# One level of Strassen's recursion for the convolution branch of an encoder block, moved with two gate blocks into a stage of its own behind the heads

## The chip, the cores and the metric

The kernel runs on one core of one Trainium2 chip. The metric is the device time of one execution in microseconds (us). The core has five engines that work side by side, each in its own order: TensorE (PE in the profile, with its weight loads as PEld), VectorE (DVE), ScalarE (ACT), GpSimd (POOL) and SyncE (SP), which here issues nearly all DMAs.

## The reference

One block of a bidirectional encoder, sequence 1024, width 1024, float32. Cut to what matters:

```python
h = rmsnorm(x, norm_w) * (1 + scale) + shift            # scale, shift, gate from silu(c) @ w_ada
(a_bg, a_cg, a_x, a_z, q, k, v, z_b, a_raw, b_raw, gate_a_raw, gate_b_raw) = split(h @ w_in)
ya = a_cg * dwconv3(a_bg * a_x) * silu(a_z);  ya = ya @ w_pa
q, k, v = silu(dwconv5([q, k, v]))                      # q, k l2-normalised, 8 heads of 128
o = gated_delta(q, k, v, g, beta) + flip(gated_delta(flip ...))   # chunked scan, both directions
yb = (rmsnorm(o) * silu(z_b)) @ w_pb
merged = sigmoid(gate_a_raw) * ya + sigmoid(gate_b_raw) * yb
return rmsnorm(x + gate * (merged @ w_o), final_norm_w)
```

## The kernel before, in words

`h` is kept transposed in SBUF: 8 tiles of 128 features x 1024 tokens, each as a rounded high part `hhi[k]` and the rest `hlo[k]`. The columns of `w_in` are taken in blocks of 128; a block's weights are loaded, and split in the same way into `wh` (ScalarE copy) and `wl` (GpSimd subtraction). One block's product is two halves of 512 tokens; a half is 8 values of k times three matmuls (`wh*hhi`, `wh*hlo`, `wl*hhi`) of 128x128 by 512. So a block is 48 matmuls. There are 80 such blocks of `w_in`: ten groups of eight, named bg, cg, ax, az (the convolution branch), q, k, v, z (the heads), ga, gb (the two gates).

The stages, in order of time:

- Start: x is loaded and normed, the first blocks k0, q0, v0 and k1 are multiplied.
- Heads: for each of 8 heads the streams `prep_k`, `prep_q`, `chain` and `head_out` do the scan. `prep_k` makes the decay matrices `D` and `N` (two buffers each: head h waits for the end of `chain` of head h-2, the mark `chain_e`), inverts 32x32 blocks on GpSimd (`E`, 30 steps of two instructions) over a round trip through DRAM, and `chain` runs the 8 chunk steps with short matmuls (`psy`, `psz`, `cb`, `o`). `fill` is a stream of block products that TensorE does whenever the chain has nothing ready: the q, k, v, z blocks of the coming heads (27 behind q1), and between them 24 gate blocks: ga, gb and az, whose results go through `activated` to DRAM (`sga_d`, `sgb_d`, `sza_d`). `choose` picks: the first 6 gates at once (`START`), the last 4 at the end (`RESERVE`), the others spread evenly over the 27.
- The order within this stage is found by the class `Scheduler`, from estimated costs and due times; it emits the instructions of all engines in that order, and each engine keeps it (`manual_schedule`). Where instructions emitted outside such a region fall among them is left to the compiler's own scheduler.
- Convolution branch: for j in 0..7 the blocks bg, ax, cg (`wtile` loads and splits weights, `product` multiplies), the width-3 convolution on VectorE (L1140, L1142), the product with `sza_d` (L1156) and the split into `yhi[j]`, `ylo[j]` (L1157, L1158), which stay in SBUF. Beside it the gate column of w_ada (`wadag`, L1144, L1146).
- pa: `ya @ w_pa`, 8 blocks over `yhi`, `ylo`; the result times `sga` goes to `m_d`. Beside it `yb_d` is read back and split into `bhi`, `blo` (L1178, L1179).
- pb: `yb @ w_pb`, 8 blocks; merged with `m_d` into `mhi`, `mlo`.
- fo: `merged @ w_o`, residual, final norm, store.

PSUM is four pools of two banks, `pp`, `pg`, `pc`, `po`. SBUF tiles of a later stage lie on bytes of earlier ones, and wait for the last use of just those tiles.

Of the kernel before, what the change touches and what calls it, by code (L numbers as in the profile page):

```python
# [15 lines left out]
P = 128  # L16
# [9 lines left out]
RESERVE = 4  # L26
# [7 lines left out]
LO_POOL = (2, 5)  # L34

# [7 lines left out]
class Slot:  # L43
    """What was done to a part of a tile: ends of reads, writes and memsets, and instructions not issued yet."""
# [6 lines left out]
class Scheduler:  # L51
    """Orders the instructions of all engines by an estimate of when they can run.

    Instructions of the engines other than TensorE are kept until their operands are there by the estimate, and then
    go to their engine by priority. Streams are generators that ask for TensorE instructions, PSUM banks, tiles and
    each other's marks; the first of them goes on whose next instruction can start at once, or else the one that can
    start first."""
# [126 lines left out]
    def step(self, stream):  # L184
        """Does what a stream asks for, and goes on to what it asks for next."""
# [65 lines left out]
class Engine:  # L251
    """Hands an engine's instructions to the scheduler."""
# [31 lines left out]
def block(ctx: ExitStack, tc: tile.TileContext, x, cT, wada, wadag, badaT, nwT, win, wab, cva, cvq,  # L284
# [10 lines left out]
    wp = pool("wp", 2)  # L295
# [22 lines left out]
    sza_d = dr.tile([8, P, T], F32, name="sza_d")  # L318
# [27 lines left out]
    def kmul(ps, w, k, half):  # L346
        wh, wl = (t[:, ch(k)] for t in w)
# [42 lines left out]
    ctx.enter_context(tc.manual_schedule(engines={nc.tensor.engine}))  # L390
    hctx = ctx.enter_context(ExitStack())
# [648 lines left out]
    def fill():  # L1040
# [11 lines left out]
        gates += [(G_B + j, f"gb{j}", activated("gb", j, sgb_d, AF.Sigmoid), []) for j in range(8)]  # L1052
        gates += [(A_Z + j, f"az{j}", activated("az", j, sza_d, AF.Silu), []) for j in range(8)]
# [33 lines left out]
    def wtile(src, name):  # L1087
        with tc.high_priority():
            hi = wp.tile([P, KT * P], F32R, tag="whi", name=f"wh_{name}")
            lo = wp.tile([P, KT * P], F32R, tag="wlo", name=f"wl_{name}")  # L1090
            for q in range(2):
                raw = wp.tile([P, 512], F32, tag="wraw", name=f"wr_{name}_{q}")
                Q.dma_start(raw, src[:, ch(q, 512)])
                S.activation(hi[:, ch(q, 512)], raw, AF.Copy)  # L1094
                G.tensor_tensor(lo[:, ch(q, 512)], raw, hi[:, ch(q, 512)].bitcast(F32), ALU.subtract)  # L1095
        return hi, lo

    def product(w, mhi, mlo, half, name):
        ps = bank((pp, pg)[half], f"pp_{name}_{half}")
        for k in range(KT):  # L1100
            wh, wl = (t[:, ch(k)] for t in w)
            sl = ch(half, 512)
            PE.matmul(ps, wh, mhi[k][:, sl], start=k == 0, stop=False)  # L1103
            PE.matmul(ps, wh, mlo[k][:, sl], start=False, stop=False)  # L1104
            PE.matmul(ps, wl, mhi[k][:, sl], start=False, stop=k == KT - 1)  # L1105
        return ps


    yctx = ExitStack()
    yp = yctx.enter_context(tc.tile_pool(name="yp", bufs=1, reuse_waits="tile", side="right"))  # L1110
    yhi = [yp.tile([P, T], F32R, name=f"yhi{k}") for k in range(KT)]
    ylo = [yp.tile([P, T], F32R, name=f"ylo{k}") for k in range(KT)]
    with tc.tile_pool(name="ap", bufs=2, reuse_waits="tile") as ap:
# [226 lines left out]
```

## Time and profile before

| | us |
|---|---|
| median of 3 runs (range) | 1516.65 (1513.97 to 1516.81) |
| span of the profiled execution | 1511.0 |
| start, up to the block v1 | 196.2 |
| heads, up to the first bg matmul | 769.4 |
| convolution branch (24 blocks) | 263.0 |
| pa (8 blocks) | 90.3 |
| pb (8 blocks) | 88.7 |
| fo and the end | 103.4 |

The page gives no time of the profiled execution beside its span, from its first to its last instruction; the median of the runs is 5.65 us more than that span. The profile lists instructions by line and tile: `pp_bg<-hhi,wh_bg` is a matmul into the PSUM tile of block group bg from `hhi` and `wh_bg`. All instructions that the scheduler of the heads emits have L200 (TensorE) or L278 (others); so groups are told apart by tile.

### The profile page before, as it was taken

Reading aid. Unit: us, or ns where it says so; the run is one execution under the profiler, and the core shown is the slowest. Engines: PE = TensorE matmul, PEld = TensorE weight load, DVE = VectorE, ACT = ScalarE, POOL = GpSimd, SP = SyncE. Lnnn points to the kernel's source line nnn. Section 1 sums busy time; section 2 is a strip of 40 time slices with the busy share of each in tenths; the row PEclk is TensorE's granted clock in tenths of the full one; section 3 lists DMA queues with packets and bytes.
Section 4 is the critical chain, followed back from the end, with each engine's and each line's share of the span. In section 5 each row is a group of like instructions: output and inputs, shape, how many; then the busy total and the mean of one; then the engine's idle time right before and its main releaser. Section 6 shows DMA issues by size and latency. Waiting matters only on the chain.

```text
span 1511.0 us, 22593 instructions
## 1 busy us (share of the span) xinstructions
PE 1433.0 (95%) x8730; PEld 1196.2 (79%) x8730; DVE 735.0 (49%) x1382; ACT 549.8 (36%) x1308; POOL 645.2 (43%) x793
## 2 busy tenths in 40 slices
PE   5999999898999999989999999999999999999898
PEld 3787878787787878878878878888888888888686
DVE  7869334664853845647628422134443344122325
ACT  5226325663553654635535424211111112122211
POOL 6213894167184392671852931222222222355401
PEclk7899999999999999999999999999999999999999
DMA  8232332223314113222132121322222137344602
GB/s 327 83 109 64 112 98 57 71 70 98 84 44 134 35 56 127 57 78 84 59 103 70 57 84 44 125 97 80 74 86 96 56 120 256 133 130 143 229 20 98
DMA packets 90298, 149.15 MB, mean 99 GB/s; under 512 B 41424, under 2 KB 41808, under 8 KB 90192
## 3 DMA queue, kind: packets, MB, share of 16 engines
q1 hardware_dynamic: 89904, 146.94, 29.6%
q8 instruction: 68, 1.11, 0.3%
q10 hardware_dynamic: 288, 0.79, 0.1%
q14 instruction: 38, 0.31, 0.1%
HBM read 118.21 MB, written 29.49 MB: 98 GB/s over the span
## 4 chain that ended last, share of the span: by engine, by line
PE 54%; DVE 9%; POOL 8%; ACT 5%; DMA 4%; issue 2%; SPq 0%; POOLq 0%; ACTq 0%
PE pp_az L200 4%; PE pp_gb L200 3%; PE cb L200 3%; PE pp_k L200 3%; DMA mr<-m_d 2%; PE o L200 2%; POOL E L278 2%; PE pp_v L200 2%; POOL et L278 2%; PE pp_cg L1103 2%; PE pp_cg L1105 2%; PE pp_cg L1104 2%; PE pp_bg L1105 2%; PE pp_ax L1105 2%; PE pp_bg L1104 2%
## 5 line engine op out<-in xcount | busy, mean ns | idle before, releaser
L278 POOL TENSOR_TENSOR E<-E,et 64x30 f32<-64x30 f32 (+14 forms) x240 | 143.9, 600 | 17.1
L278 POOL TENSOR_TENSOR et<-E 64x30 f32<-64x30 f32 (+14 forms) x240 | 135.2, 564 | 17.2
L1138 DVE TENSOR_TENSOR axp<-pp_ax,bg 128x512 f32<-128x512 f32 x16 | 11.1, 692 | 111.1 <-PE pp_ax L1105 90.5
L278 ACT ACTIVATE vw<-cb,cols 128x128 f32<-128x128 f32 x112 | 36.2, 365 | 76.1 <-PE cb L200 75.7
L278 ACT ACT_TABLE_LOAD x47 | 60.3, 1283 | 1.6 <-PEq L1335 0.8
L278 DVE SCALAR_TENSOR_TENSOR vT<-xpad,cvq_t,vT 128x1024 f32<-128x1024 f32 x32 | 58.6, 1831 | 1.0
L1095 POOL TENSOR_TENSOR wl_ax<-wr_ax,wh_ax 128x512 fp32r<-128x512 f32 x16 | 27.3, 1724 | 68.2 <-ACT wh_ax L1094 68.2
L278 POOL TENSOR_TENSOR wl_q<-wr_q,wh_q 128x512 fp32r<-128x512 f32 x16 | 22.0, 1390 | 72.2 <-ACT wh_q L278 67.4
L200 PE MATMUL pp_z<-hhi,wl_z 128*128 128x512 f32 x128 | 52.2, 408 | 0.0
L200 PE MATMUL pp_z<-hhi,wh_z 128*128 128x512 f32 x128 | 52.2, 407 | 0.0
L200 PE MATMUL pp_gb<-hlo,wh_gb 128*128 128x512 f32 x128 | 51.9, 406 | 0.0
L200 PE MATMUL pp_ga<-hhi,wh_ga 128*128 128x512 f32 x128 | 51.8, 405 | 0.0
L200 PE MATMUL pp_gb<-hhi,wh_gb 128*128 128x512 f32 x128 | 51.8, 405 | 0.0
L200 PE MATMUL pp_z<-hlo,wh_z 128*128 128x512 f32 x128 | 51.7, 404 | 0.0
L200 PE MATMUL pp_az<-hhi,wl_az 128*128 128x512 f32 x128 | 51.7, 404 | 0.0
L200 PE MATMUL pp_az<-hhi,wh_az 128*128 128x512 f32 x128 | 51.7, 404 | 0.0
L200 PE MATMUL pp_gb<-hhi,wl_gb 128*128 128x512 f32 x128 | 51.6, 403 | 0.0
L200 PE MATMUL pp_az<-hlo,wh_az 128*128 128x512 f32 x128 | 51.4, 402 | 0.0
L200 PE MATMUL pp_ga<-hlo,wh_ga 128*128 128x512 f32 x128 | 51.3, 401 | 0.0
L200 PE MATMUL pp_ga<-hhi,wl_ga 128*128 128x512 f32 x128 | 51.2, 400 | 0.0
L1104 PE MATMUL pp_pa<-ylo,wh_pa 128*128 128x512 f32 x128 | 50.8, 397 | 0.2 <-DVE ylo L1158 0.2
L1095 POOL TENSOR_TENSOR wl_pa<-wr_pa,wh_pa 128x512 fp32r<-128x512 f32 x16 | 21.9, 1388 | 68.1 <-ACT wh_pa L1094 68.1
(352 smaller groups left out, 4490.5 us busy)
## 6 DMA issues: line engine op xcount, KB each, us to landing
wada<-in_wada SPq DMA_DIRECT2D x16, 512.0 KB, 7.3
D<-gr_d SPq DMA_DIRECT2D x16, 512.0 KB, 5.9
xt<-in_x SPq DMA_DIRECT2D x8, 512.0 KB, 7.8
wr_k<-in_win SPq DMA_DIRECT2D x16, 256.0 KB, 2.6
wr_q<-in_win SPq DMA_DIRECT2D x16, 256.0 KB, 3.5
wr_v<-in_win SPq DMA_DIRECT2D x16, 256.0 KB, 2.6
wr_ga<-in_win SPq DMA_DIRECT2D x16, 256.0 KB, 2.9
qg<-er_d SPq DMA_DIRECT2D x8, 512.0 KB, 6.2
```

The costliest lines, as they stand in the source:

```text
L200: getattr(self.pe, what)(out, *ins, **kw)
L278: self._sched.record(self._name, lambda: real(*args, **kw), outs, ins, cost, extra, table, op == "memset")
L1095: G.tensor_tensor(lo[:, ch(q, 512)], raw, hi[:, ch(q, 512)].bitcast(F32), ALU.subtract)
L1103: PE.matmul(ps, wh, mhi[k][:, sl], start=k == 0, stop=False)
L1104: PE.matmul(ps, wh, mlo[k][:, sl], start=False, stop=False)
L1105: PE.matmul(ps, wl, mhi[k][:, sl], start=False, stop=k == KT - 1)
L1138: V.tensor_tensor(xp[:, 1 + 512 * half : 513 + 512 * half], ps, bg[:, ch(half, 512)], ALU.mult)
```

## The change

1. az leaves the heads, and so do gb4 to gb7: `fill` has 12 gates (ga0 to ga7, gb0 to gb3) in place of 24. `RESERVE` goes from 4 to 3. `sza_d` goes.
2. Behind the heads comes a new stage, whose VectorE, ScalarE, GpSimd and SyncE instructions are in an order written out (`manual_schedule`). First the blocks gb4 and gb5, multiplied as before (`PLAIN = (4, 6)`). Beside them `sums(m)`, m in 0..3, forms four combinations `T1` to `T4` of quarters of h (even and odd k, first and second 512 tokens), each split into high and low: 64 KB of each partition.
3. Then 17 pairs of blocks: bg, ax, cg, az for j = 0, 2, 4, 6, and gb6 with gb7. A pair is a 2x2 product of quarters, done by seven products in place of eight (Winograd's form): a product is 12 matmuls of 128x128 by 512 into one bank, a pair 84 matmuls in place of 96. `prep` (five products ahead) makes each product's weights: a VectorE sum for four of the seven, a ScalarE copy, a GpSimd subtraction. `after` and `consume` bring the banks together on VectorE: `e1` (ScalarE copy), `u2`, `u3`, and an addition for three of the four quarters of the result. S3 adds into the bank that `u2` must have read.
4. The convolution (`conv3`, six instructions for a pair) is spread over the products behind ax, two for each product. The first pair and the last have their products in another order (`plain`).
5. The branch's result goes to DRAM (`y_d`), and at the start of pa it is read back in 8 tiles through two buffers (`yr`) and split into `yhi`, `ylo`, which lie on the bytes of `hhi`, `hlo`.
6. The gate column (`wadag`) moves from the convolution branch into pa. In pa and pb, left and right sides of SBUF are swapped. The blocks' k order in DRAM becomes 0, 2, 4, 6, 1, 3, 5, 7 (`KORDER`).

The diff, cut to its core:

```diff
-RESERVE = 4
+RESERVE = 3
+PLAIN = (4, 6)
+AHEAD = 5
+KORDER = (0, 2, 4, 6, 1, 3, 5, 7)
...
-        gates += [(G_B + j, f"gb{j}", activated("gb", j, sgb_d, AF.Sigmoid), []) for j in range(8)]
-        gates += [(A_Z + j, f"az{j}", activated("az", j, sza_d, AF.Silu), []) for j in range(8)]
+        gates += [(G_B + j, f"gb{j}", activated("gb", j, sgb_d, AF.Sigmoid), []) for j in range(PLAIN[0])]
...
+    yrp = ctx.enter_context(tc.tile_pool(name="yrp", bufs=2, reuse_waits="tile", side="right"))
+    tctx.enter_context(tc.manual_schedule(engines=others))
+    def sums(m):
+        t = []
+        for k in (2 * m, 2 * m + 1):
+            t.append(yrp.tile([P, T], F32, tag="yr", name=f"hx{k}"))
+            (V if k % 2 else G).tensor_tensor(t[-1], hhi[k].bitcast(F32), hlo[k].bitcast(F32), ALU.add)
+        b11, b12, b21, b22 = (x[:, ch(half, 512)] for x in t for half in range(2))
+        V.tensor_tensor(b11, b12, b11, ALU.subtract)
+        V.tensor_tensor(b12, b22, b12, ALU.subtract)
+        V.tensor_tensor(b22, b22, b11, ALU.subtract)
+        V.tensor_tensor(b21, b21, b22, ALU.subtract)
+        for n, x in zip(SUMS, (b11, b22, b12, b21)):
+            hi, lo = hop[n][m]
+            S.activation(hi, x, AF.Copy)
+            (G if n == "T3" else V).tensor_tensor(lo, x, hi.bitcast(F32), ALU.subtract)
+    RHS = {"S2": "T2", "A11": "B11", "S1": "T1", "S3": "T3", "A12": "B21", "A22": "T4", "S4": "B22"}
+    BANK = {"S2": pg, "A11": pp, "S1": pc, "S3": pg, "A12": pp, "A22": pg, "S4": pc}
+    class Pair:
+            self.order = ("A11", "S4", "S2", "A12", "S1", "S3", "A22") if plain else tuple(RHS)
+        def prep(self, n):
+            t = self.operand(n if n in ADDS else (int(n[1]) - 1, int(n[2]) - 1))
+            S.activation(hi, t, AF.Copy)
+            G.tensor_tensor(lo, t, hi.bitcast(F32), ALU.subtract)
+        def after(self, n, ps):
+            if n == "A11":
+                self.temp("e1", ps, None)
+            if n == ("S2" if self.plain else "A11"):
+                self.temp("u2", self.banks[pg], u["e1"])
+            if n == "S3":
+                self.temp("u3", ps, u["e1"])
+                self.consume(1, 1, self.banks[pc], u["u3"])
+            elif n == "A12":
+                self.consume(0, 0, ps, None)
+            elif n == "A22":
+                self.consume(1, 0, ps, u["e1"])
+            elif n == ("S1" if self.plain else "S4"):
+                self.consume(0, 1, ps, u["u2"])
+    def mixed(name, j0, plain=False):
        def consume(b, half, ps, add):
            if add is not None:
                V.tensor_tensor(t, ps, add, ALU.add)
            if name == "ax":
                V.tensor_tensor(x, t, x, ALU.mult)
                if seen[b] == 2:
                    late.extend((acc, b, j0 + b, i) for i in range(3))
...
    pairs = [mixed(n, j, (n, j) == ("bg", 0)) for j in range(0, 8, 2) for n in ("bg", "ax", "cg", "az")]
+    pairs += [stored("gb", j, sgb_d, AF.Sigmoid, j == 6) for j in range(PLAIN[1], 8, 2)]
+    for i, (p, n) in enumerate(steps):
+        if i + AHEAD < len(steps):
+            q, k = steps[i + AHEAD]
+            q.prep(k)
+        p.product(n)
+        for _ in range(min(2, len(late))):
+            conv3(*late.pop(0))
...
+    for k in range(KT):
+        raw = yrp.tile([P, T], F32, tag="yr", name=f"yr{k}")
+        Q.dma_start(raw, y_d[k])
+        S.activation(yhi[k], raw, AF.Copy)
+        V.tensor_tensor(ylo[k], raw, yhi[k].bitcast(F32), ALU.subtract)
```

More of the change, by code (lines that the diff above doesn't have):

```diff
@@ L1096, in wtile, with product @@
         return hi, lo
-    def product(w, mhi, mlo, half, name):
+    def product(w, mhi, mlo, half, name, order=tuple(range(KT))):
         ps = bank((pp, pg)[half], f"pp_{name}_{half}")
-        for k in range(KT):
-            wh, wl = (t[:, ch(k)] for t in w)
+        for i, k in enumerate(order):
+            wh, wl = (t[:, ch(i)] for t in w)
             sl = ch(half, 512)
-            PE.matmul(ps, wh, mhi[k][:, sl], start=k == 0, stop=False)
+            PE.matmul(ps, wh, mhi[k][:, sl], start=i == 0, stop=False)
@@ new lines, in stored, with consume @@
+    def stored(name, j0, dst, func, plain=False):
+        outs = {}
+        def consume(b, half, ps, add):
+            if b not in outs:
+                outs[b] = [bt.tile([P, T], F32, tag="out", name=f"{name}{j0 + b}", bufs=3), 0]
+            o, sl = outs[b][0], ch(half, 512)
+            if add is not None:
+                V.tensor_tensor(o[:, sl], ps, add, ALU.add)
+                ps = o[:, sl]
+            S.activation(o[:, sl], ps, func)
+            outs[b][1] += 1
+            if outs[b][1] == 2:
+                Q.dma_start(dst[j0 + b], o)
+        return Pair(name, j0, consume, plain)
@@ new lines, in conv3 @@
+    def conv3(acc, b, j, i):
+        x, c = xpads[b][:, 1 + i : 1 + i + T], cva_t[:, j, i : i + 1]
+        if i:
+            V.scalar_tensor_tensor(acc, x, c, acc, ALU.mult, ALU.add)
+        else:
+            V.tensor_scalar(acc, x, c, None, ALU.mult)
+    pairs = [mixed(n, j, (n, j) == ("bg", 0)) for j in range(0, 8, 2) for n in ("bg", "ax", "cg", "az")]
+    pairs += [stored("gb", j, sgb_d, AF.Sigmoid, j == 6) for j in range(PLAIN[1], 8, 2)]
+    steps = [(p, n) for p in pairs for n in p.order]
@@ new lines, in block @@
+    plain = range(*PLAIN)
+    ws = [wtile(win[G_B + plain[0]], f"gb{plain[0]}")]
+    for i, j in enumerate(plain):
+        for m in range(4 * i // len(plain), 4 * (i + 1) // len(plain)):
+            sums(m)
+        if j + 1 in plain:
+            ws.append(wtile(win[G_B + j + 1], f"gb{j + 1}"))
+        if j + 1 not in plain:
+            for p, n in steps[:AHEAD]:
+                p.prep(n)
+        xp = xpads[i % 2]
+        for half in range(2):
+            ps = product(ws[i], hhi, hlo, half, f"gb{j}", KORDER)
+            S.activation(xp[:, 2 + 512 * half : 514 + 512 * half], ps, AF.Sigmoid)
+        Q.dma_start(sgb_d[j], xp[:, 2 : T + 2])
@@ new lines, in block, with gate_column @@
+    bctx = ExitStack()
+    bp = bctx.enter_context(tc.tile_pool(name="bp", bufs=1, reuse_waits="tile", side="right"))
+    bhi = [bp.tile([P, T], F32R, name=f"bhi{k}") for k in range(KT)]
+    blo = [bp.tile([P, T], F32R, name=f"blo{k}") for k in range(KT)]
+    psm = bank(pc, "psg")
+    gsum = []
+    def gate_column(j):
+        PE.matmul(psm[:, j : j + 1], gsum[j], one)
+        V.tensor_tensor(gcol[:, j : j + 1], psm[:, j : j + 1], badaT_t[:, 16 + j : 17 + j], ALU.add)
+    with tc.tile_pool(name="bs", bufs=2, reuse_waits="tile", side="right") as bs:
@@ L1140, in block @@
-            V.tensor_scalar(acc, xp[:, 0:T], cva_t[:, j, 0:1], None, ALU.mult)
-            for i in range(1, 3):
-                V.scalar_tensor_tensor(acc, xp[:, i : i + T], cva_t[:, j, i : i + 1], acc, ALU.mult, ALU.add)
-            ga = ap.tile([P, P], F32, tag="ga", name=f"ga{j}")
+                ps = product(w, yhi, ylo, half, f"pa{j}")
+                V.tensor_tensor(sg[:, ch(half, 512)], ps, sg[:, ch(half, 512)], ALU.mult)
+            Q.dma_start(m_d[j], sg)
+            ga = bs.tile([P, P], F32, tag="ga", name=f"ga{j}")
```

197 lines of the change are left out of this document (125 added, 72 removed).

## The prediction

> **What bounds the kernel now.** I read the page's first lines, then the busy time by stage, then single stretches.
>
> ```profile
> span 1511.0 us, 22593 instructions
> PE 1433.0 (95%) x8730; PEld 1196.2 (79%) x8730; DVE 735.0 (49%) x1382; ACT 549.8 (36%) x1308; POOL 645.2 (43%) x793
> ```
>
> ```profile
> core 0: us, PE busy (x) PEld busy (x) DVE busy (x) ACT busy (x) POOL busy (x), PEclk, DMA share, GB/s
> 196.20:965.60 769.40, 729.25 (x5570) 618.06 (x5569) 403.11 (x849) 363.60 (x965) 395.55 (x538) 0.98 0.25 77
> 965.60:1228.60 263.00, 263.00 (x1168) 217.85 (x1166) 105.80 (x140) 44.22 (x72) 68.76 (x52) 1.00 0.24 82
> 1228.60:1318.90 90.30, 90.09 (x388) 72.48 (x387) 27.93 (x27) 18.63 (x26) 22.72 (x17) 1.00 0.55 195
> ```
>
> TensorE is busy through the branch and pa, and all but 40 us of the heads, where filler covers the chain. So time is TensorE work. Its pace stands in the chain that ended last, in its last stretch of filler; the starts of the stages are in the order of time:
>
> ```profile
> 479.33 0.68 PE psy L200 x50
> ...
> 579.57 0.68 PE psy L200 x50
> ...
> 942.41 23.36 PE pp_az L200 x103
> ```
>
> ```profile
> 196.33 0.39 PE L200 MATMUL pp_v<-hhi,wh_v 128*128 128x512 f32 x1
> ...
> 965.61 0.39 PE L1103 MATMUL pp_bg<-hhi,wh_bg 128*128 128x512 f32 x1
> ...
> 1228.60 0.40 PE L1103 MATMUL pp_pa<-yhi,wh_pa 128*128 128x512 f32 x1
> ```
>
> 23.36 / 103 = 0.2268 us a matmul; a block of 48 is 10.88 us, a Strassen product of 12 is 2.72, a pair of 84 is 19.05. The first bg and the first pa matmul give the branch's 263.0 us; the two `psy` lines, the same step of head 3 and head 4, give a head's time now, 100.2 us.
>
> **The change, part by part.** *Matmuls.* The heads lose 12 blocks: -130.6. Two plain blocks come: +21.8. 17 pairs come: +323.8. The branch goes: -263.0. Together -48.0 us; all else is what it costs to get them.
>
> *Heads, +4 (-10 to +25).* From v1's first matmul at 196.3 to 965.6 stand 27 main blocks and the 18 gates that follow the first six, 45 x 10.88 = 489.6; the other 279.7 us, chain, preparation and idle, are 35.0 a head. With four main blocks a head then takes 43.5 + 35.0 = 78.5 us. Latency must allow that. The last head:
>
> ```profile
> 788.85 0.50 PE L200 MATMUL pp_k<-hhi,wl_k 128*128 128x512 f32 x1
> ...
> 825.25 0.15 POOL L278 MEMSET E<- 64x32 f32 x1 [3.48 <-DMA E<-s]
> ...
> 876.27 0.27 POOL L278 TENSOR_TENSOR E<-E,et 64x30 f32<-64x30 f32 x1
> ...
> 883.77 0.24 PE L200 MATMUL psy<-T,N 32*32 32x32 f32 x2
> ...
> 938.61 1.64 POOL L278 TENSOR_TENSOR oss<-oss,pos_half 128x8 f32<-128x8 f32 x1 [4.29 <-DVE oss L278]
> ...
> 941.38 0.38 PE L200 MATMUL otp<-ident,vp 128*128 128x128 f32 x2
> ```
>
> From the last k matmul to `otp` are 152.5 us. `D` and `N` have two buffers, so two heads share it: 76.3 us a head, just under 78.5. At the end, behind k7, come q7, v7, z6, z7 and four gates (the spread reaches two of its three places before `jobs` is empty), 87 us, with two heads' 70 of other work: 157, against 152.5. It fits closely; I take 4 us for the loss of cover. The high end is the first rival below; the low end would need a quarter of the 40 idle microseconds to go with the filler that they stand beside.
>
> *Entry to the new stage, +5 (0 to +16).* Durations:
>
> ```profile
> L1095 POOL TENSOR_TENSOR wl_bg<-wr_bg,wh_bg 128x512 fp32r<-128x512 f32 x14 | 17.9, 1297 | 58.3 <-ACT wh_bg L1094 58.3
> L1094 ACT ACTIVATE wh_bg<-wr_bg 128x512 fp32r<-128x512 f32 x14 | 8.1, 624 | 64.7 <-PE pp_ax L1104 64.7
> L1134 ACT ACTIVATE bg<-pp_bg 128x512 f32<-128x512 f32 x16 | 9.4, 588 | 14.4 <-PE pp_bg L1105 14.4
> L1138 DVE TENSOR_TENSOR axp<-pp_ax,bg 128x512 f32<-128x512 f32 x16 | 11.1, 692 | 111.1 <-PE pp_ax L1105 90.5 <-DMA wr_bg<-in_win 11.1 <-PE psg L1122 9.5
> L1251 DVE TENSOR_TENSOR y<-y,t 128x512 f32<-128x512 f32 (+1 forms) x17 | 11.8, 692 | 0.6
> L1140 DVE TENSOR_SCALAR acc<-axp,cva_t 128x1024 f32<-128x1024 f32 x8 | 13.4, 1671 | 0.1
> L1142 DVE SCALAR_TENSOR_TENSOR acc<-axp,cva_t,acc 128x1024 f32<-128x1024 f32 x16 | 21.3, 1333 | 0.2
> L278 DVE SCALAR_TENSOR_TENSOR vT<-xpad,cvq_t,vT 128x1024 f32<-128x1024 f32 x32 | 58.6, 1831 | 1.0
> ```
>
> ```profile
> L1140 DVE TENSOR_SCALAR acc<-axp,cva_t x8: 1006/1796/1797, 990.2 to 1218.5; 128x1024 f32<-128x1024 f32 x8
> ```
>
> One `sums(m)`: GpSimd adds 1024 columns (2 x 1.30), VectorE subtracts four times 512 (2.8), ScalarE copies, VectorE and GpSimd take the low parts (about 2.1 on the path); the two `yr` buffers keep the next m from starting early: about 8.5 us, 34 for four. The preparation of A11 is behind `sums(3)` on ScalarE and GpSimd, +1.9. Plain gb4 and gb5 cover 21.8. By the order of allocation parts of `T2` lie on head 7's `vp`, which `otp` reads last, so little runs ahead of 941. If TensorE has no gate left by then, 34 + 1.9 - 21.8 = 14, or with stretched instructions 16, stay open; each gate behind `otp` takes 10.9 off. I take 5.
>
> *VectorE behind each ax pair, +14 (+8 to +28).* A22 of ax ends at 0, then S4, and cg's S2, A11, S1 end at 2.7, 5.4, 8.2, 10.9. VectorE's order: add and multiply (1.4), two convolution instructions (3.0), add and multiply again, the other four (5.7), the sum for cg's S4 (0.7): 12.3 with hops of about 0.2. ScalarE copies that sum before `e1` (0.62 + 0.59), then `u2` (0.69): 14.4. S3, due at 10.9, overwrites what `u2` reads. So 3.5 us, four times. The low end has the convolution at its quickest (1.01 and about 1.27: 1.9 us left), the high end at 1.8 each with the multiplications stretched too (6.9). This wait stands in every j; nothing is behind it on TensorE that could go ahead. The sums, `u2` and `u3` of other pairs end inside a 2.72 us product: nothing. In the two plain pairs A22 follows S3 at once and waits for `u3`: 2 x 1.1, +2 (+1 to +3). The weights' loads are as many bytes as before, on the same queue, and wait only for buffers of the pair before the last; the stores of `y_d` take the place of those of `sza_d`. GpSimd has 7 x 1.30 = 9.1 and ScalarE 7 x 0.62 + 4 x 0.59 = 6.7 of 19.05 us: covered, five products ahead.
>
> *Reading y back, +14 (+8 to +22).* Before, pa began at once. Now 8 tiles of 512 KB go through two buffers:
>
> ```profile
> wada<-in_wada SPq DMA_DIRECT2D x16, 512.0 KB, 7.3
> ...
> az<-sza_d SPq DMA_DIRECT2D x8, 512.0 KB, 4.2
> ...
> ybr<-yb_d SPq DMA_DIRECT2D x8, 512.0 KB, 5.8
> ```
>
> ```profile
> L1157 ACT ACTIVATE yhi<-acc 128x1024 fp32r<-128x1024 f32 x7 | 7.4, 1062 | 13.8 <-DVE acc L1156 13.8
> L1158 DVE TENSOR_TENSOR ylo<-acc,yhi 128x1024 fp32r<-128x1024 f32 x7 | 8.6, 1226 | 7.9 <-ACT yhi L1157 7.9
> ```
>
> The first two can wait loaded, but are split only when gb6's fourth product has read odd k of `hhi`, three products (8.2 us) before pa. A buffer's turn is 4.2 to 5.8 + 1.06 + 1.23 + hops 0.7 = 7.2 to 8.8 us. Tile 7 is the second buffer's fourth: split at -5.4 + 3 x (7.2 to 8.8) = 16 to 21 us. The first half of pa0 ends 0.7 behind it, the second 5.4 later, at 22 to 27 in place of 10.9: 11 to 16. Middle 14.
>
> *The rest, +1 (0 to +5).* `wadag`, 8 x 512 KB more in pa, whose DMA share is 0.55; the gate column is 8 short instructions a block beside 28 us of VectorE in 90. fo's wait stays:
>
> ```profile
> L1245 PE MATMUL fo<-woh,mhi 128*128 128x512 f32 x92 | 36.9, 401 | 6.4 <-ACT mhi L1219 6.4
> ```
>
> The new k order costs nothing where weights come a block ahead; the start could lose 1 us.
>
> The clock: the Trainium skill, "TensorE: Matmul & The Clock Gate", Part 1, says that an idle window of some 3.4 us halves the array's clock until a busy one; by it each long wait above would add about 1.7 us, some 3 in all. The page's granted clock agrees in sign: 0.98 in the heads, where TensorE has gaps, 1.00 in the branch. The sum does without it.
>
> **Sum.** -48.0 + 4 + 5 + 14 + 2 + 14 + 1 = -8.0 us: a span of 1503. The median of the runs, 1516.65, is 5.65 above the profiled span; 1508.65, say 1508.5. With all terms but the heads at their low ends and those at 0: -48 + 17 = -31, 1485.5. The high ends have each their own rival below.
>
> **Rivals.**
>
> *The heads do not shrink (slower).* 76.3 us a head by latency is 2 us under the work. With filler gone the same conversions, inversions and chain steps stand closer on VectorE (403 us of 769, then of some 640), so each step of the chain finds it busy more often. If 152.5 becomes 164, a head takes 82, 3.5 more for six heads: +21, 1529.5. It decides at 79.8 us a head, where the 8 us are gone. Against it: the chain already runs with filler between its steps.
>
> *VectorE and GpSimd hinder each other (slower).* The same 1024 columns take 2.19 us while GpSimd works, 1.23 when it is done:
>
> ```profile
> 998.99 3.54 POOL L1095 TENSOR_TENSOR wl_ax<-wr_ax,wh_ax 128x512 fp32r<-128x512 f32 x2 [8.29 <-ACT wh_ax L1094]
> ...
> 999.18 2.19 DVE L1156 TENSOR_TENSOR acc<-acc,az 128x1024 f32<-128x1024 f32 x1
> 1002.50 1.23 DVE L1158 TENSOR_TENSOR ylo<-acc,yhi 128x1024 fp32r<-128x1024 f32 x1 [1.13 <-ACT yhi L1157]
> ```
>
> In the new stage GpSimd is busy half the time, in the sums nearly all. If most such instructions are stretched by 0.5 to 0.9 us, the ax wait is 6.9 (+14) and the entry 16 (+11): 1533.5. The Trainium skill, "SBUF — State Buffer", section "SBUF: two separate sides", has the rule: VectorE with two SBUF inputs and GpSimd lock one port pair for a whole instruction. The trace agrees, 2.19 against 1.23. Against the rival: operands from PSUM keep 0.69.
>
> *The waits eat all of it (same).* At pa's start the loads of `wadag`, `sga`, `ybr` and the weights come too, as bytes come free. Landings of 8 us, where the `wada` loads of the crowded start took 7.3, make y's turn 11 us: tile 7 is split at -5.4 + 33 = 27.6, pa0 ends at 33.7, 22.8 late: +8 or 9, 1517.
>
> *Cover is better than I see (much faster).* All low ends, 1485.5: the chain runs as deep as now, the sums run ahead of `otp`, and the loads land in 4.2.
>
> **Chances.** Forecast, 1490 to 1512: 0.50. Much faster: 0.05. Same: 0.12. Heads slower: 0.19. VectorE and GpSimd: 0.14. So faster 0.55, same 0.12, slower 0.33; 0.2% (3 us) is about what runs of this kernel tell apart. The range takes 1487 to 1533; the likeliest case alone is 1490 to 1512.
>
> **What would show it.** 17 x 12 = 204 matmuls of 512 columns fewer. The heads' end near 840. `u2` on the chain of waits at cg's S3, about 3.5 us, four times. A gap in pa0 with `ylo` as releaser, about 14 us. Under 25 us of TensorE idle from the first plain block to the first pa matmul would bear the sum out. A head above 80 us, A11 more than 15 us late, or another wait in every pair (seventeen times what I count for ax alone) would make it wrong; so would a stall in every product, as each hangs on a weight preparation of three engines.

## The result, and the profile after

The changed kernel takes 1584.6 us (median of 4 runs, 1581.1 to 1585.8), the one before 1516.0 on the same chip: ratio 1.044, 95% interval 1.041 to 1.046. It is slower, where 1508.5 was forecast, and lies above the range's 1533. The profiled span grew by 72.0 us, the medians are 68.6 apart (the profile of before, 5.0 us under its median, is a quick one), and TensorE's busy time did not fall, though 204 matmuls are gone (8730 to 8526). The page's first lines of the changed kernel:

```profile
span 1583.0 us, 22634 instructions
...
PE 1436.9 (91%) x8526; PEld 1185.9 (75%) x8526; DVE 874.4 (55%) x1577; ACT 569.7 (36%) x1360; POOL 739.1 (47%) x848
```

Its busy time by stage: heads from v1 to the first plain block; plain blocks and first pair; the other sixteen pairs; from the end of the pairs to pb.

```profile
core 0: us, PE busy (x) PEld busy (x) DVE busy (x) ACT busy (x) POOL busy (x), PEclk, DMA share, GB/s
197.10:889.90 692.80, 621.98 (x4994) 525.70 (x4993) 395.35 (x854) 308.83 (x895) 380.08 (x515) 0.94 0.23 67
889.90:946.80 56.90, 46.19 (x182) 36.07 (x181) 35.60 (x39) 20.22 (x37) 34.72 (x21) 0.91 0.27 93
946.80:1277.60 330.80, 317.47 (x1345) 257.28 (x1343) 187.26 (x217) 92.14 (x150) 139.06 (x107) 0.97 0.18 63
1277.60:1389.30 111.70, 98.65 (x402) 77.76 (x401) 59.49 (x101) 26.36 (x35) 25.75 (x20) 0.91 0.64 221
```

The first number is the length, the one before the DMA share the granted clock of TensorE. Every stage has TensorE idle and a clock below 1.00; before, the branch and pa had neither. TensorE's waits in the changed kernel, the longest of each part:

```profile
PE otp L203 <- DVE vp L281: 16.1, 4, 13.5
PE ps_cg_S L1188 <- DVE u_cg L1197: 12.5, 4, 3.1
...
PE ps_bg_A L1188 <- ACT whA_bg L1174: 5.6, 1, 5.6
PE pp_pa L1106 <- ACT yhi L1318: 5.3, 2, 4.5
PE pp_pa L1106 <- ACT wh_pa L1097: 5.3, 1, 5.3
```

Against the terms of the forecast:

| term | forecast | measured | how |
|---|---|---|---|
| matmuls | -48.0 | -48.0 | 204 fewer instructions; work by the forecast's pace |
| heads | +4 | +55 | end at 889.9, before 965.6: -75.7 instead of -130.6 |
| entry and first pair | +5 | +16 | 56.9 us for 21.8 + 19.05 of work |
| the other pairs | +16 | +26 | 330.8 us for 16 x 19.05 = 304.8 |
| y and pa0 | +14 | +19 | last matmul before pa to the first of pa1: 31.0, before 12.0 |
| rest | +1 | +4 | pa1 to the end |
| sum | -8 | +72 | |

The heads alone turn the sign. The same stretch in both kernels, from the first k1 matmul to the end of the heads, first before and then after:

```profile
95.00:966.00 871.00, 827.61 (x6038) 698.71 (x6037) 469.32 (x969) 413.24 (x1078) 455.06 (x626) 0.99 0.26 81
```

```profile
95.00:890.00 795.00, 720.97 (x5458) 607.21 (x5457) 460.46 (x973) 357.66 (x1006) 441.24 (x603) 0.95 0.24 73
```

Idle TensorE is length less busy time: 43.4 us before, 74.0 after. The busy time fell by 106.6, while 576 matmuls of 0.2268 us fewer are 130.6. So some 31 us went into idle time and some 24 into matmuls that ran slower. The granted clock fits the 24: the time by which it falls short of full speed, the stretch's length times one minus the clock, is 12 us before (0.986) and 41 after (0.949), part of it in idle time. The slices of 100 us show that the two lie together, first before, then after:

```profile
500.00:600.00 100.00, 95.53 (x732) 81.25 (x730) 58.94 (x123) 52.16 (x136) 55.20 (x77) 1.00 0.25 80
600.00:700.00 100.00, 94.55 (x718) 79.86 (x718) 57.15 (x119) 51.23 (x130) 56.60 (x77) 1.00 0.26 80
```

```profile
500.00:600.00 100.00, 86.81 (x893) 74.47 (x894) 66.41 (x151) 49.40 (x157) 55.69 (x78) 0.90 0.24 68
600.00:700.00 100.00, 88.89 (x683) 74.44 (x682) 53.83 (x128) 41.67 (x123) 51.83 (x87) 0.91 0.22 64
```

Before, 5 us of each 100 are idle and the clock stays at 1.00; after, 11 to 13 are idle and the clock stands at 0.90 and 0.91. What a long wait looks like, in order of time in the changed kernel:

```profile
790.50 0.47 PE L203 MATMUL pp_z<-hhi,wl_z 128*128 128x512 f32 x1
...
816.32 2.15 PE L203 MATMUL otp<-ident,vp 128*128 128x128 f32 x8 [13.49 <-DVE vp L281]
...
818.11 0.78 PE L203 MATMUL pp_z<-hhi,wh_z 128*128 128x512 f32 x1
```

z6 ends at 790.5; z7, next in the filler's list, needs out(6), and the three gates still there are held back (`RESERVE = 3`). So no filler stands beside the end of the chain of head 6, and z7 starts on half the clock. Head 3's output was late too, though its chain was done at 570.8 (`oss`): its `otp` came only at 615.5 (why, is not shown), and z4, which needs it, held up the list, so that no filler ran from 589 to 617.

### The profile page after: what moved, and what is told of

Its sections match the earlier page's. It is cut to its first block, busy times and chain, and to the rows that moved or that the text cites. A ratio compares the mean times of both kernels' runs of the same rounds, so it can differ in the third digit from the quotient of the medians.

```text
span 1583.0 us, 22634 instructions
## 1 busy us (share of the span) xinstructions
PE 1436.9 (91%) x8526; PEld 1185.9 (75%) x8526; DVE 874.4 (55%) x1577; ACT 569.7 (36%) x1360; POOL 739.1 (47%) x848
## 4 chain that ended last, share of the span: by engine, by line
PE 54%; DVE 18%; POOL 10%; DMA 7%; ACT 6%; issue 4%; SPq 1%; POOLq 0%; ACTq 0%; DVEq 0%
PE cb L203 4%; PE pp_k L203 4%; PE ps_bg_S L1188 3%; PE ps_az_S L1188 3%; POOL E L281 3%; DVE kT L281 3%; PE ps_ax_S L1188 3%; POOL et L281 3%; PE pp_z L203 3%; PE o L203 3%; PE ps_cg_S L1188 3%; DMA mr<-m_d 2%; PE pp_v L203 2%; ACT sqj L281 2%; DVE D L281 2%
## 5 line engine op out<-in xcount | busy, mean ns | idle before, releaser
L281 DVE SCALAR_TENSOR_TENSOR S<-S,exps,cb 128x128 f32<-128x128 f32 x96 | 30.1, 342 | 78.3 <-PE cb L203 77.9
L1106 PE MATMUL pp_pa<-yhi,wh_pa 128*128 128x512 f32 x128 | 53.6, 419 | 10.6 <-ACT yhi L1318 5.3
L1108 PE MATMUL pp_pa<-yhi,wl_pa 128*128 128x512 f32 x128 | 52.6, 411 | 0.6 <-POOL wl_pa L1098 0.6
L1175 POOL TENSOR_TENSOR wlS_cg<-S_cg,whS_cg 128x512 fp32r<-128x512 f32 x16 | 20.6, 1286 | 63.3 <-ACT whS_cg L1174 63.2
L1106 PE MATMUL pp_pb<-bhi,wh_pb 128*128 128x512 f32 x128 | 49.9, 390 | 0.0
L1108 PE MATMUL pp_pb<-bhi,wl_pb 128*128 128x512 f32 x128 | 49.9, 390 | 0.0
L1107 PE MATMUL pp_pb<-blo,wh_pb 128*128 128x512 f32 x128 | 49.9, 389 | 0.0
L281 DVE SCALAR_TENSOR_TENSOR kT<-xpad,cvq_t,kT 128x1024 f32<-128x1024 f32 x32 | 49.5, 1548 | 0.5
L281 DVE SCALAR_TENSOR_TENSOR r<-cb,negeg,vp 128x128 f32<-128x128 f32 x112 | 35.0, 345 | 26.0 <-PE cb L203 25.8
L281 ACT ACTIVATE vn<-cb,cols 128x128 f32<-128x128 f32 x128 | 41.8, 372 | 17.5 <-PE cb L203 17.4
```

What stands on the lines that cost most here:

```text
L281: self._sched.record(self._name, lambda: real(*args, **kw), outs, ins, cost, extra, table, op == "memset")
L1106: PE.matmul(ps, wh, mhi[k][:, sl], start=i == 0, stop=False)
L1108: PE.matmul(ps, wl, mhi[k][:, sl], start=False, stop=i == KT - 1)
L1175: G.tensor_tensor(lo, t, hi.bitcast(F32), ALU.subtract)
```

## The experiments

Two theories of the heads at first. T1: the filler is one list taken in order; a z that waits for an output stops what is behind it, and TensorE runs dry. T2: with less filler the latency round a head (conversion, GpSimd's inversion, chain) is what counts. T3 is the second rival of the prediction: VectorE and GpSimd hinder each other. T4 came with the runs that change a constant: the order that the planner finds is a draw. "Stretch" is from the first k1 matmul to the end of the heads; by work it should be 870.4 - 130.6 = 739.8 with (4, 6). e1 to e14 are one run each, and repeated runs of the kernel before lie between 1513 and 1523 us, so the readings go by stretches of the traces. Where two runs have the same heads, their stretches lie 2 to 7 us apart (after and e4, 795.3 and 793.7; e1 and e12, 774.8 and 768.2).

**e1: another order of the filler.**

```diff
+                jobs.append((Z0 + h - 2, f"z{h - 2}", silu_z(h - 2), [("out", h - 3)] if h > 2 else []))
                 jobs.append((V0 + h, f"v{h}", conv(h, "v", 16, "tmp", 2), [("pq", h - 1)]))
-                jobs.append((Z0 + h - 1, f"z{h - 1}", silu_z(h - 1), [("out", h - 2)] if h > 1 else []))
```

> In the filler's list z(h-1) no longer stands right behind v(h) but one head later, in front of v(h+1); nothing else changes. Heads are measured from the first v1 matmul to the first matmul of the plain block gb4: 692.8 us in the changed kernel, 643 by the prediction. T1 (the filler is one list taken in order, and a z that waits for the output of the head before it holds up the k and q behind it): heads 15 to 50 us shorter, TensorE's waits on otp mostly gone, k3 starts some 40 us earlier. T2 (the ring of two D/N buffers and the GpSimd inversion bound the heads): heads within 8 us of 692.8.

Heads 672.3 us, 20.5 shorter; the waits on `otp` fell from 16.1 to 4.3 us, k3 starts at 315.9 instead of 373.7; 1557.1 us in all. That is what T1 expected, and T2 in its strict form falls. But other waits grew (TensorE waited 15.6 us before `gram`, 3.0 in the changed kernel), and the stretch is 774.8, still 35 over the work. Nor do 20 us show the list as their cause: e3 below gained more by another order alone, with 14.8 us of waits on `otp` left. For the list speaks that the nine runs with it lie 22 to 35 us over their work, while of the three orders without it two lie at +55 and one at +26.

**e2: the inversion cut short**, and **e5: the same in the kernel before.**

```diff
+        V.tensor_scalar(bk, bk, 0.001, None, ALU.mult)
         V.tensor_scalar(nbk, bk, -1.0, None, ALU.mult)
...
-        for p in range(1, 31):
+        for p in range(1, 3):
```

> Leaves out 28 of the 30 steps of each head's 32x32 inversion on GpSimd, and scales beta by 0.001 so that the numbers stay small; all else is done. The inversion took 45 to 64 us of each head. T2 (latency round a head's ring): heads fall from 692.8 to 660 or less, and more than the reordered filler list of the other run gives. T1 (order of the filler): heads fall by less than 15, and the late outputs of heads 2 and 3 stay.

> The kernel before with 28 of the 30 inversion steps left out and beta scaled by 0.001, as was done with the changed one (where the heads ended 57 us earlier). T2 (before, the filler covers the inversion; with twelve blocks less it shows): the heads here end within 12 us of before's, at about 965 us, and the run takes 1505 to 1520. Rival (the inversion costs both kernels time, through VectorE and GpSimd sharing or through its length): they end 40 us or more earlier and the run takes under 1480.

The same window, the changed kernel and then the one before:

```profile
95.00:833.00 738.00, 695.21 (x5462) 589.04 (x5461) 447.76 (x985) 366.59 (x1017) 180.52 (x157) 0.99 0.27 78
```

```profile
95.00:948.00 853.00, 821.81 (x6037) 692.68 (x6036) 450.39 (x977) 412.48 (x1076) 219.22 (x178) 0.99 0.27 82
```

Without the inversion's time the stretch of the changed kernel is 738, what its work asks for, with before's idle time (42.8) and before's clock (0.99): 57 us gone. Before loses 17.8, between the two expectations, nearer T2's 12. So about 40 us of the 55, give or take the spread of the orders below (29 us), hang on the inversion, which the filler of before covered for the most part and the thinner one does not. The cut takes latency, GpSimd's load (441 to 181 us) and its traffic beside VectorE away together; which of them counts is not told apart here.

**e3 and e9: the same work in another order; e8 and e10: the same for the kernel before.** Only the planner's estimate of a hop changes:

```diff
-HOPS = {'same': 0.15, 'other': 0.2, 'from pe': 0.4, 'to pe': 0.35}
+HOPS = {'same': 0.16, 'other': 0.2, 'from pe': 0.4, 'to pe': 0.35}
```

> One constant of the planner is changed, the estimate of a hop between two instructions of the same engine from 0.15 to 0.16 us: no work is added or removed, only the order of the instructions may fall out differently. T4 (the order of the changed kernel is an unlucky draw: with less filler the order depends on small margins): heads at least 12 us shorter than 692.8, with other heads late or none. T1 and T2 in their strict form: heads within 8 us of 692.8.

> The changed kernel with the planner's estimate of a hop on the same engine 0.14 instead of 0.15 us: the same work, a third order of it. From the first k1 matmul to the first plain gb4 matmul the changed kernel took 795.3 us, of them 74.0 with TensorE idle; before took 870.4 with 43.4 idle, and 576 matmuls of 0.2268 us lie between, so that 739.8 was due. T4 with the clock (each us idle over before's 43 costs 1.5 to 1.9 us, since the clock is halved behind a long wait): the stretch is 740 + 1.5 to 1.9 times (idle - 43), and lies between 760 and 800. Rival (matmuls are slower for another reason, contention in SBUF): the stretch doesn't follow the idle time.

> The kernel before with the planner's estimate of a hop on the same engine 0.14 instead of 0.15 us: the same work in another order. T4 (only with less filler does the order depend on small margins): within 5 us of before. Rival (any order of this planner is a draw, and before's was a lucky one): 8 us or more slower.

> The kernel before with 0.18 instead of 0.15 us, a third order of its work. If before's own order was a lucky one: 1522 to 1535, the heads' end 8 to 18 us later than 965.6. If the order that was slower was the unlucky one: within 5 us of before.

| run | stretch | idle | over its work | over per us of more idle |
|---|---|---|---|---|
| before | 870.4 | 43.4 | | |
| e10, before, 0.18 | 876.2 | 42.6 | +6 | |
| e8, before, 0.14 | 886.8 | 52.0 | +16 | 1.9 |
| after | 795.3 | 74.0 | +55 | 1.8 |
| e9, after, 0.14 | 795.2 | 77.8 | +55 | 1.6 |
| e3, after, 0.16 | 766.1 | 59.6 | +26 | 1.6 |
| e1, list | 774.8 | 65.8 | +35 | 1.6 |
| e2, short inversion | 737.5 | 42.8 | -2 | |

The order is a draw in both kernels (29 us over three orders of the changed one, 16 before), but luck is not the cause: two of three draws lie at +55, and the best at +26. T4 explains spread, not level. e3 and e9 came out as T4 had them, and e10 as if the slower order were the unlucky one; e8's T4 (within 5 us) fell. The last column is the find: a microsecond of additional idle time cost 1.6 to 1.9 us, and in the later runs 1.4 to 1.9. Two runs don't follow: e10 (6 us without more idle) and e13 (29 us for 9). Their clock accounts for e10 and for part of e13: 0.977 and 0.969 over the stretch, so 9 and 12 us more short of full speed than before.

**e4: one step of convolution behind a product.**

```diff
-        for _ in range(min(2, len(late))):
+        for _ in range(min(1, len(late))):
```

> One step of the deferred convolution behind each product instead of two, so that VectorE is less busy when cg's S3 waits for u2. Theory of the pairs (VectorE's queue): the four waits of 3.1 to 3.3 us before cg's S3 go, and with them the half clock behind them; the four cg pairs fall from about 25 to 19.3 us each, the stage from first pair to last falls by 18 to 24 us. Rival (GpSimd and VectorE hinder each other, each operation is longer): the waits move to a later product and the stage falls by under 8 us. Heads unchanged in both, within 2 us of 692.8.

Heads 692.6; first pair to last 334.3 instead of 355.0, every cg pair 19.3, as the first expectation had it. The stage's 20.7 us are 12.5 of wait and some 8 of clock. The wait in the changed kernel, as the forecast had described it:

```profile
974.11 0.39 PE L1188 MATMUL ps_cg_S<-T1h,wlS_cg 128*128 128x512 f32 x1
...
976.87 0.69 DVE L1197 TENSOR_TENSOR u_cg<-ps_cg_S,e_cg 128x512 f32<-128x512 f32 x1 [1.26 <-ACT e_cg L1195]
...
977.62 0.80 PE L1188 MATMUL ps_cg_S<-T3h,whS_cg 128*128 128x512 f32 x1 [3.12 <-DVE u_cg L1197]
...
979.06 0.63 PE L1188 MATMUL ps_cg_S<-T3h,whS_cg 128*128 128x512 f32 x1
```

After 3.12 us of waiting, matmuls of the same shape take 0.63 us in place of 0.39 (the first 0.80) and follow each other at 0.43 instead of 0.23. The granted clock is 0.50 for 6.8 us behind this wait, and for 3.4 behind each of the other three.

**e6: more gates in the heads; e7: four edits together.** Both have e1's list. e6:

```diff
-PLAIN = (4, 6)
+PLAIN = (6, 8)
-AHEAD = 5
+AHEAD = 3
...
-            ps = yield get(po, f"otp{h}_{half}", os_)
+            ps = yield get(pg, f"otp{h}_{half}", os_)
...
-    yrp = ctx.enter_context(tc.tile_pool(name="yrp", bufs=2, reuse_waits="tile", side="right"))
+    yrp = ctx.enter_context(tc.tile_pool(name="yrp", bufs=4, reuse_waits="tile", side="right"))
```

> On top of the reordered filler list: otp takes its bank from pg instead of po; six gb blocks in the heads instead of four, gb6 and gb7 plain, no gb pair (PLAIN = (6, 8)); and, in another stage, four buffers for the y read back instead of two, paid for with three products' weights ahead instead of five. Heads, against the run with (4, 6) beside it: if TensorE's own work bounds them, two more blocks cost 21 to 24 us; if latency does (T2), under 12. From the end of the last pair to the end of pa0: 30 us in the changed kernel; if the two buffers hold the reading back, 20 to 24; if it is the release of hhi and hlo, 28 to 32.

e7 has e4's line, this `otp` line, and in the entry:

```diff
+        if i == 0:
+            for p, n in steps[:2]:
+                p.prep(n)
         for m in range(4 * i // len(plain), 4 * (i + 1) // len(plain)):
             sums(m)
...
-            for p, n in steps[:AHEAD]:
+            for p, n in steps[2:AHEAD]:
                 p.prep(n)
```

> Reordered filler list, otp from pg, one convolution step behind each product, and the weights of the first two products prepared ahead of the sums of h. Heads: T1 says 640 to 665 us from v1 to gb4 (the bank was the other half of the lateness of out(h)), T2 says 665 to 680, as with the list alone. Pairs: 334 as with one convolution step alone. From the first plain block to the first pair: 32.7 in the changed kernel; 22 to 27 if the weights of A11 and S4 were late because they stood behind the sums on ScalarE and GpSimd.

e7: stretch 767.7, heads 666.6, pairs 334.1, span 1535.2 (1537.1 us). The heads came out where T2 had them, not T1. The bank of `otp` added nothing that can be told: e1 without it has 774.8, but e12 below, also without it, 768.2. e6's stretch is 783.7, 16 us for two more blocks of 10.9: between the two expectations, so it decides nothing. From the end of the pairs to pa1 e6 took 34.4, longer with four buffers; but there no gb pair covers the last store of y. Only e16 and e17 below told this apart. The entry was a miss: 32.5 again. The wait had moved from A11's weights to gb5's, which stood behind the sums on ScalarE (`wh_gb`, 6.9 us).

**e11: all weights ahead of the sums, and yb later.** Else as e7.

```diff
+        if j + 1 in plain:
+            ws.append(wtile(win[G_B + j + 1], f"gb{j + 1}"))
+        for p, n in steps[2 * i : (2, AHEAD)[i]]:
+            p.prep(n)
         for m in range(4 * i // len(plain), 4 * (i + 1) // len(plain)):
             sums(m)
...
-            raw = bs.tile([P, T], F32, tag="raw", name=f"ybr{j}")
+            for b in range(max(0, 2 * j - 8), max(0, 2 * j - 6)):
+                raw = bs.tile([P, T], F32, tag="raw", name=f"ybr{b}")
```

> As the kernel with the four edits together, and in two other stages: gb5's weights and the first products' operands are now prepared ahead of the sums of h (there only two products' were, and gb5's weights stood behind the sums), and the yb tiles are loaded in the second half of the pa stage, two for each block from pa4 on. From the first plain block to the first pair, 32.5 there: 23 to 27 if order on ScalarE alone was the cause; 30 or more with the wait moved to the first pair if the sums themselves (some 40 us on VectorE and GpSimd, in a row) are too long. From the end of the pairs to the end of pa0, some 31 there: 20 to 24 if yb's and the other loads hold up y's on the DMA engines; 28 to 32 if the release of hhi and hlo does.

The plain blocks took 21.8 us, and the wait came back in the first pair, now for the sums themselves:

```profile
PE ps_bg_S L1189 <- ACT T2h L1136: 10.5, 2, 6.5
```

From the first plain block to the first ax pair 60.9 us, 4 more than in the changed kernel. So the order on ScalarE is not the cause; the length of the four sums is, from the first addition to the last low part 40.0 us in e7 and 45.0 here. y stayed at 31.7, but this says nothing of yb's loads: though the program has them later, the first one still goes out at 1240.0 us, just ahead of pa0's first matmul at 1240.3, as in the changed kernel (1282.3 and 1283.2).

**e12: the sums on VectorE alone.**

```diff
-            (V if k % 2 else G).tensor_tensor(t[-1], hhi[k].bitcast(F32), hlo[k].bitcast(F32), ALU.add)
+            V.tensor_tensor(t[-1], hhi[k].bitcast(F32), hlo[k].bitcast(F32), ALU.add)
...
-            (G if n == "T3" else V).tensor_tensor(lo, x, hi.bitcast(F32), ALU.subtract)
+            V.tensor_tensor(lo, x, hi.bitcast(F32), ALU.subtract)
```

> The reordered filler list, and all of the sums of h and their low parts on VectorE, none on GpSimd. In the changed kernel VectorE's add of two tiles of 1024 columns takes 1.21 us alone and 3.27 beside GpSimd's. T3 (the two engines hinder each other): the four sums take 30 to 34 us instead of 40 and the stretch from the first plain block to the end of the first pair falls by 4 to 8 us, against 26.9 + 24 with the list alone. Rival (VectorE's own queue is the limit): no gain, or 2 to 6 us more.

From the first plain block to the first ax pair 45.4 us; e1, which has the same list, took 50.8. T3 holds here: one engine is quicker than two. Part of the gain is that the additions of the first sum ran at 41 us, in the start; but each of the other three took 8.6 us, where in e1 they took 9.3 to 11.0, and in e17 below all four took 35.1 where e7 has 40.0. The addition of two tiles in the changed kernel, on VectorE's timeline: alone, then begun 0.16 us ahead of GpSimd's, then begun 0.50 us behind it:

```profile
872.12 1.22 DVE L1127 TENSOR_TENSOR hx<-hhi,hlo 128x1024 f32<-128x1024 f32 x1
...
894.15 1.21 DVE L1127 TENSOR_TENSOR hx<-hhi,hlo 128x1024 f32<-128x1024 f32 x1
...
914.91 3.30 DVE L1127 TENSOR_TENSOR hx<-hhi,hlo 128x1024 f32<-128x1024 f32 x1
```

and GpSimd's own, at the same places:

```profile
894.31 3.30 POOL L1127 TENSOR_TENSOR hx<-hhi,hlo 128x1024 f32<-128x1024 f32 x1 [0.63 <-DVE T4l L1136]
...
914.41 2.72 POOL L1127 TENSOR_TENSOR hx<-hhi,hlo 128x1024 f32<-128x1024 f32 x1
```

So the addition that began second took 3.30 us on either engine.

**e13 and e14: the inversion on VectorE**, in the changed kernel and in the one before.

```diff
-            G.tensor_tensor(tt, E[:, 0:p, p : p + 1].to_broadcast([64, p, n]),
+            V.tensor_tensor(tt, E[:, 0:p, p : p + 1].to_broadcast([64, p, n]),
...
-            G.tensor_tensor(E[:, 0:p, p + 1 :], E[:, 0:p, p + 1 :], tt, ALU.add)
+            V.tensor_tensor(E[:, 0:p, p + 1 :], E[:, 0:p, p + 1 :], tt, ALU.add)
```

> The changed kernel with the 60 small instructions of each head's inversion on VectorE instead of GpSimd (where they took 42 to 64 us a head, 33 to 46 of them their own). T2 (latency round the ring of a head): if they take under 30 us a head there, the stretch from k1 to gb4 falls from 795 to 740 to 770, idle from 74 to 45 to 60. Rival (VectorE, 57% busy in the heads, is the next bound, or the order of the filler is the cause): 780 or more.

> The same in the kernel before. T2 (there the filler hides most of the inversion): the heads end 5 to 20 us earlier than at 965.6, as with 28 steps left out (18), the run at 1497 to 1512. Rival (VectorE becomes the bound): no gain or slower.

Stretch 768.8 with 52.4 idle in e13, 892.9 with 56.7 in e14: the changed kernel gains 26 us, the one before loses 22. e13 landed on its first expectation, but e14 shows the rival at work, and a gain of 26 is also what another order gave. An inversion still spans 34 to 47 us in e13, since VectorE's other work gets in between (its own instructions take 20 to 23). This didn't settle the share of latency.

**e15: together; e16: with two more gates.** Both have e1's list, `otp` from `pg`, and the edits of e4, e12 and e13; e16 also:

```diff
-PLAIN = (4, 6)
+PLAIN = (6, 8)
```

> Changed kernel with all that helped: reordered filler list, otp from pg, one convolution step behind each product, the sums of h and the inversion on VectorE. By the runs so far: 1583 - 28 (heads, list and bank) - 21 (convolution) - 10 (sums) = 1524, and 10 to 25 less if the shorter inversion adds to the order of the filler: span 1499 to 1514. If the list and the inversion cure the same idle time: 1520 to 1526.

> The run with all together and PLAIN = (6, 8): two gb blocks more in the heads, the last gb pair gone (19.3 us). If the heads still have idle time and half clock to fill: heads +8 to +15, span 4 to 11 us shorter than with (4, 6). If TensorE's work bounds them now: heads +22, span 0 to 6 longer, and the reading back of y, whose last store no gb pair covers, up to 4 more.

e15: 1530.9 us, ratio to before 1.008 (1.007 to 1.010), stretch 765.6. The inversion on VectorE adds nothing to the list's gain (e7: 767.7): list and inversion cure the same idle time, as the second expectation had it, though the profiled span, 1529.1, lies 3 us above the 1520 to 1526 expected. e16 is slower, 1.018 (1.016 to 1.021): two blocks cost 26.5 us in the stretch, more than their 21.8, and y without a gb pair behind it takes 41.0 us to pa1 against 32.4 (e6, without that pair too but with four buffers, took 34.4). The span is 12.8 us longer than e15's, past both expectations.

**e17: four buffers for y, and room for pa0's weights; e18: its work in another order.** The inversion is back on GpSimd; otherwise as e15, with:

```diff
-AHEAD = 5
+AHEAD = 3
...
-    yrp = ctx.enter_context(tc.tile_pool(name="yrp", bufs=2, reuse_waits="tile", side="right"))
+    yrp = ctx.enter_context(tc.tile_pool(name="yrp", bufs=4, reuse_waits="tile", side="right"))
...
-    for i, n in enumerate(SUMS):
+    for n in ("T2", "T1", "T3", "T4"):
         hop[n] = [[tp.tile([P, 512], F32R, name=f"{n}{p}{m}") for p in "hl"] for m in range(4)]
```

> Reordered filler list, otp from pg, one convolution step, sums of h on VectorE (the inversion is back on GpSimd), and for y: four yr buffers instead of two with three products' weights ahead instead of five, and T2's tiles laid where pa0's weights come to lie later, since T2 is done with two products earlier than T1. If the two buffers hold y up: from the end of the pairs to the end of pa0 14 to 20 us instead of 31, with the wait for pa0's weights (5.4) gone, and the span 1508 to 1516, so 1.00 of before. If the release of hhi and hlo does: 27 to 31 and the span 1522 to 1530.

> The same with the planner's estimate of a hop on the same engine 0.16 instead of 0.15 us. If the mended list has taken the luck out of the order: heads within 8 us of the run with 0.15. If not: 10 to 30 us apart, either way.

e17: 1515.7 us (12 runs) against 1518.0, ratio 0.998, interval 0.997 to 1.000: level with before, just under it. e18: 1.001 (0.999 to 1.002), stretch 764.5 against 767.2; its heads are within 3 us of e17's, as the first expectation had it, though this is one more order and no more. From the end of the pairs to pa1 19.0 us in place of 31.0, as expected if the two buffers hold y up. The traces show how. With two buffers the last two loads of y go out only when a tile has been split, behind the first of pa's other loads, and take 10.5 and 9.7 us to land, where the four before them took 3.5 to 5.4. The last one on SyncE's timeline, changed kernel:

```profile
1288.62 0.33 SPq L1317 DMA_DIRECT2D yr<-y_d  x1
```

and in e17, where the last two are out before those others and land within 6.5 us:

```profile
1213.68 1.48 SPq L1318 DMA_DIRECT2D yr<-y_d  x2
```

In both kernels ScalarE converts each of the later tiles as soon as it has landed, so the conversions of yb that stand between them cost nothing. Its timeline, changed kernel:

```profile
1284.96 1.06 ACT L1318 ACTIVATE yhi<-yr 128x1024 fp32r<-128x1024 f32 x1 [1.26 <-DMA yr<-y_d]
1291.20 1.06 ACT L1353 ACTIVATE bhi<-ybr 128x1024 fp32r<-128x1024 f32 x1 [5.17 <-DMA ybr<-yb_d]
...
1294.97 1.06 ACT L1318 ACTIVATE yhi<-yr 128x1024 fp32r<-128x1024 f32 x1
...
1298.31 1.06 ACT L1318 ACTIVATE yhi<-yr 128x1024 fp32r<-128x1024 f32 x1 [0.66 <-DMA yr<-y_d]
```

and e17:

```profile
1208.48 3.89 ACT L1319 ACTIVATE yhi<-yr 128x1024 fp32r<-128x1024 f32 x4
...
1221.41 1.04 ACT L1319 ACTIVATE yhi<-yr 128x1024 fp32r<-128x1024 f32 x1
1222.36 1.14 ACT L1098 ACTIVATE wh_pa<-wr_pa 128x512 fp32r<-128x512 f32 x2
```

Four tiles stand loaded when the memory comes free, and the last is converted 13 us after the first, not 29. Fewer weights ahead and the place of T2 came with the buffers, so the runs alone do not separate the three. The wait for pa0's weights (4.5 of 5.3 us) stayed: moving T2's tiles had little effect. The stages of e17, to be read against those of the changed kernel:

```profile
95.00:862.10 767.10, 706.80 (x5459) 599.74 (x5458) 476.89 (x980) 371.65 (x1019) 445.68 (x602) 0.96 0.25 75
862.10:907.20 45.10, 42.23 (x182) 33.43 (x181) 30.98 (x40) 17.36 (x31) 15.90 (x12) 1.00 0.31 105
907.20:1218.20 311.00, 308.86 (x1345) 251.97 (x1343) 193.44 (x220) 93.31 (x154) 147.64 (x109) 1.00 0.22 74
1218.20:1317.90 99.70, 93.84 (x403) 75.52 (x401) 60.91 (x99) 23.07 (x33) 25.13 (x19) 0.97 0.66 229
```

Of 69.1 us regained 27.8 are the heads', 11.8 the entry's and first pair's, 19.8 the other pairs', 11.9 those of y and pa0; the rest gave 2 back. Once next to nothing waits in the Strassen stage its clock is 1.00. e17's span is still 51 us above before's less the 48 saved; 27 of them are in the heads (767.1 over 739.8), and what causes these 27 is not shown.

## Why the prediction was wrong

**Matmuls, -48.0: right.** 204 instructions are gone. Where nothing waits a pair takes 19.3 us instead of 19.05, which makes 4 us over sixteen pairs, counted with the pairs below.

**Heads, +4: the step that failed, by 51 us.** The forecast held the latency of a head, half of 152.5 us, to be covered by the filler that is left, 78.5 us of work a head. Three things were wrong with it.

- *The measure of cover.* The 152.5 us from the last k matmul to `otp` were taken from head 7, the last, with the least work beside it. In the same trace heads 2 to 6 took 173 to 182, so 86 to 91 a head by the two buffers' rule, well over the 78.5. But the interval is no bound either way: after the change, heads 2 to 6 took 162 to 220, and in e17, whose stretch is 28 us shorter, 197 to 245. It holds waits for the list of filler and stretches with it. What shows the cover are the runs with the inversion cut short: 57 us came back in the changed kernel and 18 in the one before, so that about 40 us of it, give or take the spread of the orders, were covered before and lie open now.
- *The list.* Each head's blocks were summed as if any of them could stand beside any chain, though z waits for an output and `RESERVE` holds gates back. The trace shows two places of 28 us without filler for this reason (589 to 617, 790 to 818). What it cost in all is not shown: e1's 20 us lie within the spread of the orders.
- *The clock.* The sum priced idle time at its length; 31 us more of it brought 24 us of slower matmuls.

How the 31 us of idle time divide between latency and list stays open; e15 shows that the gains of the two edits do not add. The first rival had the mechanism (heads that shrink less, for latency), with +21 for a size that was +51 beyond the sum's 4, and had 0.19 of the chances.

**Entry, +5: 16, the end of its range.** The last sum ended 34 us behind the heads' end (889.9 to 923.9), though the first had run ahead of it; four sums took 40.0 us in e7, not 34, as additions were stretched beside GpSimd's: the second rival's mechanism, in the place and of the size it named. The forecast's own formula gave 14 to 16 if TensorE has no gate left behind `otp`, and but for the last 5 us of one it had none; the choice of 5 was the error. The rival did not hold for the ax waits: those were 3.1 us, not 6.9.

**VectorE behind each ax pair, +14: place, count and length right** (four times `u2`, 3.1 us against 3.5); with the clock behind it it cost 20.7. **Reading y back, +14: 19**, inside its range. The mechanism, a buffer's turn, was right; the last two turns were long because the loads took 10 us among pa's others, as the rival "The waits eat all of it" had feared with 8.

**The clock.** The prediction cited the Trainium skill, "TensorE: Matmul & The Clock Gate", Part 1, for an estimate of about 1.7 us behind each long wait, some 3 us in all, and left it out of the sum. The total was too low for its own list of waits: the four behind ax make 6.8. In size e4 bears the rule out: 20.7 us back for 12.5 of waits, 2 us a wait on top, against 1.7. But these waits were 3.1 us long, a little shorter than the window of some 3.4 that the page gives, and the clock was halved all the same. What was wrong above all was to count a few long waits and no heads, where most of the idle time lay.

## What to carry to other kernels

Work taken out of a stage that it fills is not worth its own length: ask what each dependent chain then has beside it, and follow the filler's list in order to see what may stand beside what. An interval that itself holds waits does not say whether the filler covers the chain; a run that leaves out the chain's longest part, done to both kernels, does. In a stage like these heads, price every additional microsecond of idle TensorE at 1.4 to 1.9 us. Where an order is planned from estimates, run two or three neutral variations first: here they spread by 16 us before and 29 after, more than the 8 us that were forecast.

## What the runs showed of the hardware that was not expected

- A VectorE add of two SBUF tiles of 1024 columns took 1.22 us alone, 1.21 when it began just ahead of GpSimd's add of the same kind, and 3.30 when it began just behind it; in the second case it was GpSimd's that took 3.30. A sum on VectorE alone took 8.6 us (e12), on both engines 9.3 to 11.0 (e1).
- After a wait of only 3.1 us a matmul of 512 columns took 0.63 us instead of 0.39, and the following ones came every 0.43 instead of 0.23; the granted clock was 0.50 for 3.4 to 6.8 us.
- Idle time and lost clock went together over the heads: 1.4 to 1.9 us for each us of idle time over before's, in all runs with more of it but e13 (3.2).
- The same load of 512 KB took 3.5 to 5.4 us from issue to landing while little else was on its way, and about 10 us beside the other loads at the start of pa.
